# A layer of attention, scan and FFN on one core: the scan's PSUM results copied out by ACT, its rotation tables built by POOL, joined with block seams by halves and grouped transposes

## The chip, the core and the metric

The kernel runs on one core of a Trainium2 chip. A core has a matrix engine (TensorE, here PE, with its weight loads as PEld), a vector engine (VectorE, DVE), an activation engine (ScalarE, ACT), GpSimd (POOL) and a queue engine (SyncE, SP) that issues most DMAs. Each engine runs its own instructions in the order in which the program has them; semaphores hold an instruction until what it needs is done. Matmul results land in PSUM, which PE, DVE and ACT reach; everything else lies in SBUF, which all engines reach. The metric is the device time of one execution in microseconds (us), the median of several.

## The reference, cut to what matters

One layer over 2048 latent tokens and 256 context tokens of width 1024: a combined input projection gives q, k, v for a neighbourhood attention, u for a bidirectional complex-diagonal scan (S5), and two gates; both branches are merged, projected and added; an FFN follows. The part that the change touches is the scan:

```python
def s5_direction(u_ctx, u_lat, lam_re, lam_im, log_dt, b_re, b_im, c_re, c_im, reverse, need_ctx):
    lb_re, lb_im, bb_re, bb_im = s5_discretise(lam_re, lam_im, log_dt, b_re, b_im)
    def drive(u):
        u = jnp.flip(u, axis=1) if reverse else u
        return (jnp.einsum('blgh,gph->blgp', u, bb_re), jnp.einsum('blgh,gph->blgp', u, bb_im))
    def readout(hr, hi):
        y = jnp.einsum('blgp,ghp->blgh', hr, c_re) - jnp.einsum('blgp,ghp->blgh', hi, c_im)
        return jnp.flip(y, axis=1) if reverse else y
    ur, ui = drive(u_ctx)
    _, _, hc_re, hc_im = diag_scan(lb_re, lb_im, ur, ui)        # h_t = lb * h_(t-1) + u_t, complex
    h0_re, h0_im = hc_re[:, -1:], hc_im[:, -1:]
    ur, ui = drive(u_lat)
    ac_re, ac_im, hl_re, hl_im = diag_scan(lb_re, lb_im, ur, ui)
    hl_re = hl_re + ac_re * h0_re - ac_im * h0_im
    hl_im = hl_im + ac_re * h0_im + ac_im * h0_re
    return None, readout(hl_re, hl_im)
# then y = gelu(y_forward + y_backward + d_skip * u), a GLU, and the merge with the attention branch
```

There are 32 channel groups of 16 channels with 64 complex states each, in two directions. All is fp32.

## The kernel before

**Order.** The program is written stage by stage, and a scheduler sorts it when it is built: each instruction has a priority (the place in the program, shifted by `tc.cur_priority`, and raised inside `with self.hot()`), and the scheduler fills each engine's row by priority and by its own estimate of when operands are ready. The order is then fixed. `s5()` (the scan) and `attention()` have the base priority; `in_proj()` (q, k, v and gates) has 100000 more, the merge and the FFN 200000 more. So the projection is what PE gets where the scan has nothing ready, the merge what it gets under the attention.

**Projection** (`in_proj`, four blocks of 512 tokens). A weight piece is loaded by SP (`raw`), cast to a high part by ACT (L70, `whi`) and reduced to a low part by DVE (L71, `wlo`); each product is three matmuls (L92 to L94). `cols` makes one 128x512 output at a time over eight pieces of the contraction. The block's inputs `n` lie in a ring of 12 buffers, eight of them per block, loaded by SP (L357). For q and k DVE applies the rotary factors (L383 to L398). At the second block POOL builds the attention biases in the same ring (`biases`, L436 to L445): eight heads, each a load from `in_rpb`, four tensor_tensor of 128x480 and three stores.

**Scan** (`s5`). Four quarters `q` of the channels, each in two batches `sb` of four groups. A batch loads its inputs by POOL's DMA queue (L651, `ut`), lets ACT reorder them (L652, `un`), transposes them on PE (per group: the context's 32 columns twice, and two 128x128) into `ug` by an ACT copy, and builds the small matrices `win`, `cl` and `mt` on DVE, PE and ACT. Then come four steps (two pairs of groups, two directions), 32 in all. A step chunks time by 8, which leaves 288 positions, and turns the complex recurrence into a real one by rotating it:

- a table of rotation factors `er`, `ei` (128x288) grows by doubling: ACT scales (L741, L742), DVE adds (L743, L744), four times;
- PE makes the chunks' inputs `pv` in PSUM (L750, one buffer of two banks); DVE multiplies them by the table straight from PSUM (L757, L758), adds (L759, L760), runs the recurrence (L762), multiplies by the table again (L765, L766) and adds into the states `h` (L771, L772).

After four steps PE makes the outputs `py` in PSUM (L780 to L782), and ACT and DVE apply the GELU (L784 to L788; both products of DVE read `py`). After a quarter the outputs are transposed and split (L795 to L799) and stored.

## Time and profile before

| | us |
|---|---|
| median of 3 runs (3228.43 to 3234.4) | 3233.86 |
| the profiled execution | 3233.39 |
| its span, first to last instruction | 3231.6 |
| PE busy in the span | 3119.2 (97%) |
| DVE busy | 2348.4 (73%) |
| ACT busy | 1570.3 (49%) |
| POOL busy | 898.9 (28%) |

The profiled execution differs from the median by 0.5 us. Matmuls are pipelined and their ends are modelled, so a busy PE isn't PE at its peak. "Busy" counts time in which at least one instruction of the engine runs. A released-by name is inferred from semaphores. The scan's stages lie between 168 and 872 us: its first small matrices are built from 168 us on, and the last outputs are split at 872 us.

### The profile page before, as it was taken

To read this page: it belongs to the slowest core of one execution; us is meant where nothing else is said; L and a number is where in the kernel's file an instruction comes from. 1 tells how busy PE (TensorE), PEld (TensorE's weight loads), DVE (VectorE), ACT (ScalarE), POOL (GpSimd) and SP (SyncE) were. 2 spreads that over 40 slices of the span, in tenths; PEclk is the share of its full clock that TensorE was granted. 3 is DMA by queue.
4 is the path that set the end of the run, shared out by engine and by line. 5 is a ranking of instruction groups with operands and counts; after the bars stand their busy time and mean duration, and the time that the engine had idled before them with its cause. 6 is when DMAs were issued, how large, how long until landed. Compare 5 with 4: busy or idle time off the path is not lost.

```text
span 3231.6 us, 54283 instructions
## 1 busy us (share of the span) xinstructions
PE 3119.2 (97%) x20600; PEld 2727.7 (84%) x20600; DVE 2348.4 (73%) x4153; ACT 1570.3 (49%) x2746; POOL 898.9 (28%) x856
## 2 busy tenths in 40 slices
PE   7999978999999998999999999999999999999998
PEld 5987766787787778788888988888989898989988
DVE  6689787897753565665657867887858966897766
ACT  4445434454355555555554444445535543554534
POOL 2000052000223232323300544742242423341243
PEclk9999989999999999999999999999999999999999
DMA  8545567454776897987847434434344434443332
GB/s 321 186 125 172 166 194 241 163 163 140 228 211 193 268 259 213 277 238 220 254 130 269 139 126 146 141 131 147 122 136 132 150 111 131 141 147 131 112 111 101
DMA packets 212853, 564.27 MB, mean 175 GB/s; under 512 B 31785, under 2 KB 63657, under 8 KB 212593
## 3 DMA queue, kind: packets, MB, share of 16 engines
q1 hardware_dynamic: 155008, 437.48, 41.2%
q0 software_dynamic: 28032, 87.64, 10.0%
q10 hardware_dynamic: 29552, 35.70, 3.2%
q8 instruction: 162, 2.65, 0.3%
q14 instruction: 99, 0.80, 0.1%
HBM read 446.95 MB, written 111.61 MB: 173 GB/s over the span
## 4 chain that ended last, share of the span: by engine, by line
PE 79%; DVE 9%; DMA 6%; issue 3%; POOL 1%; ACT 1%; SPq 0%; ACTq 0%; DVEq 0%; POOLq 0%
PE ps L92 15%; PE ps L94 15%; PE ps L93 15%; PE ps L1068 8%; PE ps L1066 8%; PE ps L1067 8%; PE o L924 3%; DVE wlo L71 3%; PE w L884 2%; PE w L905 1%; DMA raw<-in_w_qk 1%; PE pv L750 1%; PE c L886 1%; PE c L907 1%; DVE n L1130 1%
## 5 line engine op out<-in xcount | busy, mean ns | idle before, releaser
L71 DVE TENSOR_TENSOR wlo<-raw,whi 128x1024 fp32r<-128x1024 f32 (+1 forms) x522 | 688.0, 1325 | 324.6 <-ACT whi L70 323.1
L70 ACT CAST whi<-raw 128x1024 fp32r<-128x1024 f32 (+1 forms) x522 | 508.3, 976 | 519.6 <-PE ps L94 185.8
L1066 PE MATMUL ps<-X,whi 128*128 128x256 f32 x2464 | 693.4, 284 | 13.2 <-DVE u L1078 8.4
L1068 PE MATMUL ps<-X,wlo 128*128 128x256 f32 x2464 | 692.4, 284 | 11.9 <-DVE wlo L71 11.7
L1067 PE MATMUL ps<-X,whi 128*128 128x256 f32 x2464 | 689.9, 283 | 0.0
L1066 PEld LDWEIGHTS ps<-X,whi 128*128 128x128 f32 x2464 | 471.2, 191 | 17.9 <-DVE u L1078 11.7
L1068 PEld LDWEIGHTS ps<-X,wlo 128*128 128x128 f32 x2464 | 470.5, 191 | 15.1 <-DVE wlo L71 14.9
L1067 PEld LDWEIGHTS ps<-X,whi 128*128 128x128 f32 x2464 | 471.3, 191 | 0.5
L92 PE MATMUL ps<-n,whi 128*128 128x512 f32 (+1 forms) x800 | 318.2, 398 | 10.3 <-ACT t L382 6.7
L93 PE MATMUL ps<-n,whi 128*128 128x512 f32 (+1 forms) x800 | 316.7, 396 | 0.0
L94 PE MATMUL ps<-n,wlo 128*128 128x512 f32 (+1 forms) x800 | 316.3, 396 | 0.5 <-DVE wlo L71 0.5
L92 PE MATMUL ps<-whi,zh 128*128 128x512 f32 x704 | 277.1, 395 | 0.0
L94 PE MATMUL ps<-whi,zl 128*128 128x512 f32 x704 | 277.0, 394 | 0.0
L93 PE MATMUL ps<-wlo,zh 128*128 128x512 f32 x704 | 276.9, 394 | 0.0
L1049 POOL TENSOR_TENSOR os<-raw 128x512 f32<-128x512 f32 x66 | 117.4, 1780 | 406.7 <-DMA raw<-in_w_f 330.7
L70 ACT CAST whi<-os 128x1024 fp32r<-128x1024 f32 x110 | 115.5, 1050 | 204.1 <-PE ps L1067 91.7
L71 DVE TENSOR_TENSOR wlo<-os,whi 128x1024 fp32r<-128x1024 f32 x110 | 151.3, 1376 | 62.9 <-ACT whi L70 62.9
L92 PEld LDWEIGHTS ps<-n,whi 128*128 128x128 f32 x800 | 151.3, 189 | 49.6 <-ACT t L382 9.0
L93 PEld LDWEIGHTS ps<-n,whi 128*128 128x128 f32 x800 | 151.5, 189 | 35.6 <-issue 4.1
L94 PEld LDWEIGHTS ps<-n,wlo 128*128 128x128 f32 x800 | 151.3, 189 | 35.0 <-issue 1.8
L1050 POOL TENSOR_TENSOR os<-raw,os 128x512 f32<-128x512 f32 x88 | 134.0, 1523 | 150.4 <-DMA raw<-in_w_f 148.5
L92 PE MATMUL ps<-y,whi 128*128 128x512 f32 x384 | 155.5, 406 | 5.1 <-DVE t L968 1.8
(343 smaller groups left out, 7098.8 us busy)
## 6 DMA issues: line engine op xcount, KB each, us to landing
raw<-in_w_f SPq DMA_DIRECT2D x198, 512.0 KB
raw<-sums SPq DMA_DIRECT2D x66, 512.0 KB
raw<-in_w_gate SPq DMA_DIRECT2D x64, 512.0 KB
raw<-in_w_f SPq DMA_DIRECT2D x66, 256.0 KB
raw<-in_w_qk SPq DMA_DIRECT2D x32, 512.0 KB
gsc<-e ACTq DMA_DIRECT2D x64, 256.0 KB
raw<-in_w_m SPq DMA_DIRECT2D x32, 512.0 KB
t<-gsc SPq DMA_DIRECT2D x64, 256.0 KB
```

Source lines behind the costliest of these rows:

```text
L70: self.nc.scalar.copy(hi, x)
L71: self.nc.vector.tensor_tensor(lo, x, hi.bitcast(F32), op=ALU.subtract)
L92: mm(ps, l[0], r[0], start=first, stop=False)
L93: mm(ps, l[0], r[1], start=False, stop=False)
L94: mm(ps, l[1], r[0], start=False, stop=last)
L884: nc.tensor.matmul(slv, q[:, qs], kl, start=(n == 0), stop=(n == 1))
L924: nc.tensor.matmul(o[h, g, :, hf, :], l, r, start=(n == 0), stop=(n == nb + 1), skip_group_check=True)
L1049: nc.gpsimd.tensor_tensor(s24[:, 0], s13[:, 0], a11, op=ALU.subtract)
L1050: nc.gpsimd.tensor_tensor(s24[:, 1], a12, s24[:, 0], op=ALU.subtract)
L1066: mm(dst, a[0][:, k], xh, start=(first and k == 0), stop=False, skip_group_check=True)
L1067: mm(dst, a[0][:, k], xl, start=False, stop=False, skip_group_check=True)
L1068: mm(dst, a[1][:, k], xh, start=False, stop=(k == 3), skip_group_check=True)
```

## The change

Five edits, four of them in the scan.

- The inputs `pv` leave PSUM by an ACT copy into `v`; `p1` and `p2` are then computed from `v`. The outputs `py` are copied by ACT into `yn`, and DVE's two products of the GELU read `yn`.
- The tables `er`, `ei` become one tile `ee` of two rows, and POOL builds them: one copy and sixteen tensor_tensor per step. ACT's ten and DVE's eight instructions for them go.
- The transposes of the inputs are grouped: the context's part once per group, four groups in one PSUM tile and one ACT copy that writes both ends of `ug`; the latent part of two groups in one tile and one copy.
- `cols` can take two neighbouring outputs as a pair: two weight pieces are loaded, and the first half of the contraction is done for both outputs before the second half. It is used for the first two k outputs of blocks 1 to 3, and for the last two outputs of the second gate of blocks 0 to 2.

```diff
-    def cols(self, pool, src, kt, c0, n, ops, tag="ps"):
+    def cols(self, pool, src, kt, c0, n, ops, tag="ps", pair=None):
         nm = 8 // kt
         for c in range(n):
+            if pair is not None and c == pair:
+                f = ops[0][1]
+                ws = [self.piece(src, 0, c0 + c + i, kt) for i in range(2)]
+                pss = [pool.tile([P, ops[0][0]], F32, name=tag) for _ in range(2)]
+                for h in range(2):
+                    for w, ps in zip(ws, pss):
+                        for k in range(h * kt // 2, (h + 1) * kt // 2):
+                            self.mm3(ps, (w[0][:, k], w[1][:, k]), f(k), k == 0, k == kt - 1)
+                for i, ps in enumerate(pss):
+                    yield c + i, 0, ps
+            if pair is not None and c in (pair, pair + 1):
+                continue
             w = self.piece(src, 0, c0 + c, kt)
...
-                for jj, i, ps in self.cols(pm, I["w_qk"], KD, c0, 4, ops):
+                for jj, i, ps in self.cols(pm, I["w_qk"], KD, c0, 4, ops, pair=0 if b and isk else None):
...
-                for m, _, ps in self.cols(pm, I["w_gate"], KD, gi * 8, 8, [lat]):
+                for m, _, ps in self.cols(pm, I["w_gate"], KD, gi * 8, 8, [lat], pair=6 if gi and b < NB - 1 else None):
...
+                    pt = psT.tile([P, NG, NCC], F32, name="pt")
                     for g in range(NG):
-                        pt = psT.tile([P, SEQC + NCC], F32, name="pt")
-                        nc.tensor.transpose(pt[:, 0:NCC], uc[:NCC, g], self.ident[:NCC, :NCC])
-                        for cb in range(2):
-                            nc.tensor.transpose(pt[:, NCC + cb * P:NCC + cb * P + P], un[cb][:, g], self.ident)
-                        nc.tensor.transpose(pt[:, SEQC:SEQC + NCC], uc[:NCC, g], self.ident[:NCC, :NCC])
-                        nc.scalar.copy(ug[:, g, :], pt)
+                        nc.tensor.transpose(pt[:, g], uc[:NCC, g], self.ident[:NCC, :NCC])
+                    ends = ug.rearrange("p g (n c) -> p g n c", c=NCC)[:, :, ::SEQC // NCC]
+                    nc.scalar.copy(ends, pt.unsqueeze(2).to_broadcast([P, NG, 2, NCC]))
+                    for g in range(0, NG, 2):
+                        pt = psT.tile([P, 2, 2, P], F32, name="pt")
+                        for j in range(2):
+                            for cb in range(2):
+                                nc.tensor.transpose(pt[:, j, cb], un[cb][:, g + j], self.ident)
+                        nc.scalar.copy(ug[:, g:g + 2, NCC:SEQC], pt.rearrange("p j c t -> p j (c t)"))
...
-                                er = pp.tile([P, SEQC], F32, name="er")
-                                ei = pp.tile([P, SEQC], F32, name="ei")
-                                nc.scalar.copy(er[:, 0:32], self.eb[:, 0, :, pr])
-                                nc.scalar.copy(ei[:, 0:32], self.eb[:, 1, :, pr])
+                                ee = pp.tile([P, 2, SEQC], F32, name="er")
+                                er, ei = ee[:, 0], ee[:, 1]
+                                G = nc.gpsimd
+                                G.tensor_copy(ee[:, :, 0:32], self.eb[:, :, :, pr])
                                 for i, m in enumerate((32, 64, 128, 256)):
                                     w = min(m, SEQC - m)
-                                    zr, zi, zn = (self.zz[:, i, x, pr:pr + 1] for x in range(3))
-                                    ea = pp.tile([P, P], F32, name="ea", bufs=1)
-                                    eb = pp.tile([P, P], F32, name="eb", bufs=1)
-                                    nc.scalar.activation(ea[:, :w], er[:, 0:w], AF.Copy, scale=zr)
-                                    nc.scalar.activation(eb[:, :w], ei[:, 0:w], AF.Copy, scale=zr)
-                                    V.scalar_tensor_tensor(er[:, m:m + w], ei[:, 0:w], zn, ea[:, :w], op0=ALU.mult, op1=ALU.add)
-                                    V.scalar_tensor_tensor(ei[:, m:m + w], er[:, 0:w], zi, eb[:, :w], op0=ALU.mult, op1=ALU.add)
+                                    zr, zi = (self.zz[:, i, x, pr:pr + 1].unsqueeze(1).to_broadcast([P, 2, w]) for x in range(2))
+                                    ea = pp.tile([P, 2, P], F32, name="ea", bufs=1)
+                                    G.tensor_tensor(ee[:, :, m:m + w], ee[:, :, 0:w], zr, op=ALU.mult)
+                                    G.tensor_tensor(ea[:, :, :w], ee[:, :, 0:w], zi, op=ALU.mult)
+                                    G.tensor_tensor(er[:, m:m + w], er[:, m:m + w], ea[:, 1, :w], op=ALU.subtract)
+                                    G.tensor_tensor(ei[:, m:m + w], ei[:, m:m + w], ea[:, 0, :w], op=ALU.add)
...
+                                with self.hot():
+                                    nc.scalar.copy(v, pv[:, :, 0:SEQC])
...
-                                V.tensor_tensor(p1, pv[:, :, 0:SEQC], two(er, SEQC), op=ALU.mult)
-                                V.tensor_tensor(p2, pv[:, :, 0:SEQC], two(ei, SEQC), op=ALU.mult)
+                                V.tensor_tensor(p1, v, two(er, SEQC), op=ALU.mult)
+                                V.tensor_tensor(p2, v, two(ei, SEQC), op=ALU.mult)
...
+                            yg = yn[cb][:, :, g0 + p0 * 2:g0 + p0 * 2 + 4].rearrange("p t g h -> p t (g h)")
+                            y2f = y2.rearrange("p t g h -> p t (g h)")
+                            nc.scalar.copy(yg, py.rearrange("p t g h -> p t (g h)"))
                             nc.scalar.activation(y2, py, AF.Square)
                             nc.scalar.activation(y2, y2, AF.Copy, scale=0.044715, bias=1.0)
-                            V.tensor_tensor(y2, y2, py, op=ALU.mult)
+                            V.tensor_tensor(y2f, y2f, yg, op=ALU.mult)
                             nc.scalar.activation(y2, y2, AF.Tanh, scale=math.sqrt(2.0 / math.pi))
-                            V.scalar_tensor_tensor(yn[cb][:, :, g0 + p0 * 2:g0 + p0 * 2 + 4].rearrange("p t g h -> p t (g h)"), y2.rearrange("p t g h -> p t (g h)"), 1.0,
-                                                   py.rearrange("p t g h -> p t (g h)"), op0=ALU.add, op1=ALU.mult)
+                            V.scalar_tensor_tensor(yg, y2f, 1.0, yg, op0=ALU.add, op1=ALU.mult)
```

The scheduler sorts the changed program anew, so rows move that the diff doesn't name. Three places follow.

DVE before, the end of the second batch's third step: table instructions (`er`, `ei`) stand between the scan's own (`p`, `h`) and the projection's (`qt`).

```order
L743 SCALAR_TENSOR_TENSOR er<-ei,zz,ea 128x128
L392 TENSOR_TENSOR qt<-t_5996,t_5997 128x4x2x32 x2
L744 SCALAR_TENSOR_TENSOR ei<-er,zz,eb 128x128
L765 TENSOR_TENSOR p_2740<-v,er 128x2x256
L766 TENSOR_TENSOR p_2741<-v,ei 128x2x256
L743 SCALAR_TENSOR_TENSOR er<-ei,zz,ea 128x32
L398 SCALAR_TENSOR_TENSOR qt<-qt 128x512
L744 SCALAR_TENSOR_TENSOR ei<-er,zz,eb 128x32
L771 TENSOR_TENSOR h_2750<-p_2740,p_2741 64x256
L772 TENSOR_TENSOR h_2750<-p_2740,p_2741 64x256
```

DVE now, the end of the same step.

```order
L71 TENSOR_TENSOR wlo<-raw,whi 128x1024
L782 TENSOR_TENSOR p_2740<-v,er 128x2x256
L783 TENSOR_TENSOR p_2741<-v,er 128x2x256
L404 TENSOR_TENSOR qt<-t_5758,t_5759 128x4x2x32 x2
L788 TENSOR_TENSOR h_2750<-p_2740,p_2741 64x256
L789 TENSOR_TENSOR h_2750<-p_2740,p_2741 64x256
```

The table's rows are gone, and the scan's own follow each other more closely.

POOL before, at the attention biases: only the biases and the scan's input loads (`ut`).

```order
L443 TENSOR_TENSOR n<-n,am 128x480
L445 DMA be<-n 128x2x320 x2
L445 DMA bi<-n 128x2x440
L442 TENSOR_TENSOR n<-am,n 128x480 x2
L443 TENSOR_TENSOR n<-n,am 128x480 x2
L445 DMA be<-n 128x2x320 x2
L436 DMA n<-in_rpb 128x1x960
```

POOL now, at the same place.

```order
L455 TENSOR_TENSOR n<-n,am 128x480
L457 DMA be<-n 128x2x320 x2
L758 TENSOR_TENSOR er<-er,ea 128x32
L759 TENSOR_TENSOR er<-er,ea 128x32
L457 DMA bi<-n 128x2x440
L454 TENSOR_TENSOR n<-am,n 128x480 x2
L751 COPY er<-eb 128x2x32
L756 TENSOR_TENSOR er<-er,zz 128x2x64
L757 TENSOR_TENSOR ea<-er,zz 128x2x64
L455 TENSOR_TENSOR n<-n,am 128x480
L448 DMA n<-in_rpb 128x1x960
```

The tables of the scan's steps stand in one row with the biases and the loads that these wait for.

PE before, the scan's last output transposes (`yn`): they stand among the 256-column matmuls of the last block's value projection.

```order
L93 MATMUL ps<-wlo,n 128x256
L94 MATMUL ps<-whi,n 128x256
L795 MATMUL pt<-ident,yn_4401 128x128 x8
L92 MATMUL ps<-whi,n 128x256
L93 MATMUL ps<-wlo,n 128x256
```

PE now: they stand among 512-column matmuls that come ahead of those.

```order
L93 MATMUL ps<-n,whi 128x512
L94 MATMUL ps<-n,wlo 128x512
L92 MATMUL ps<-n,whi 128x512
L814 MATMUL pt<-ident,yn_4257 128x128 x8
L93 MATMUL ps<-n,whi 128x512
L94 MATMUL ps<-n,wlo 128x512
```

The end of the scan has moved ahead in PE's row: 267 matmuls of 512 columns and 33 of 256 that stood before it stand behind it.

## Rows read from the trace of the kernel before

**Rows 1.** The page's first part: engine, busy us (share of the span), instructions.

```profile
PE 3119.2 (97%) x20600; PEld 2727.7 (84%) x20600; DVE 2348.4 (73%) x4153; ACT 1570.3 (49%) x2746; POOL 898.9 (28%) x856
```

**Rows 2.** Busy us (instructions) by stretch: PE, PEld, DVE, ACT, POOL; granted clock, DMA.

```profile
168.00:340.00 172.00, 170.65 (x1042) 142.07 (x1041) 153.76 (x335) 87.13 (x196) 8.23 (x10) 1.00 0.50 152
340.00:551.00 211.00, 183.84 (x951) 144.18 (x951) 169.09 (x300) 82.89 (x172) 67.57 (x70) 0.94 0.64 201
551.00:724.00 173.00, 172.66 (x950) 138.19 (x949) 149.49 (x298) 86.68 (x177) 4.77 (x6) 1.00 0.52 169
724.00:872.00 148.00, 148.00 (x785) 116.00 (x784) 121.01 (x239) 67.98 (x138) 14.88 (x28) 1.00 0.52 167
...
400.00:530.00 130.00, 105.61 (x570) 85.17 (x569) 109.38 (x182) 45.94 (x97) 64.46 (x66) 0.91 0.64 191
```

**Rows 3.** Waits, 388 to 560 us: engine, line, released by, total us, times, longest.

```profile
POOL n L442 <- DMA n<-in_rpb: 53.6, 7, 11.3
...
ACT un L652 <- DMA ut<-us: 18.0, 2, 10.6
...
PE pv L750 <- DVE p L758: 9.0, 2, 7.2
```

**Rows 4.** Timeline of PE in the scan: start us, us, instruction.

```profile
388.04 0.40 PE L92 MATMUL ps<-n,whi 128*128 128x512 f32 x1
...
392.24 0.40 PE L92 MATMUL ps<-n,whi 128*128 128x512 f32 x1
```

**Rows 5.** Busy time by stretch of line L743, then of L744.

```profile
168.00:872.00 704.00, 37.01 (x128) 0.98 0.55 174
...
168.00:872.00 704.00, 38.07 (x128) 0.98 0.55 174
```

**Rows 6.** Groups by line and shape, 150 to 910 us: count, busy us, mean ns.

```profile
L757 DVE TENSOR_TENSOR p<-pv,er 128x576 f32<-128x576 f32 x32 | 24.1, 753 | 1.8 <-PE pv L750 1.5
...
L765 DVE TENSOR_TENSOR p<-v,er 128x512 f32<-128x512 f32 x32 | 22.0, 686 | 0.2
```

**Rows 7.** Groups of DVE by line and shape, 400 to 530 us.

```profile
L71 DVE TENSOR_TENSOR wlo<-raw,whi 128x1024 fp32r<-128x1024 f32 x13 | 18.8, 1442 | 9.8 <-ACT whi L70 9.8
L772 DVE TENSOR_TENSOR h<-p,p 64x256 f32<-64x256 f32 x8 | 8.1, 1017 | 0.1
...
L743 DVE SCALAR_TENSOR_TENSOR er<-ei,zz,ea 128x64 f32<-128x64 f32 x5 | 2.1, 425 | 0.0
```

**Rows 8.** Groups of DVE by line and shape, 552 to 850 us.

```profile
L71 DVE TENSOR_TENSOR wlo<-raw,whi 128x1024 fp32r<-128x1024 f32 x41 | 50.1, 1221 | 17.6 <-ACT whi L70 17.2
...
L772 DVE TENSOR_TENSOR h<-p,p 64x256 f32<-64x256 f32 x32 | 13.5, 421 | 0.5
...
L743 DVE SCALAR_TENSOR_TENSOR er<-ei,zz,ea 128x64 f32<-128x64 f32 x14 | 3.9, 278 | 0.0
```

**Rows 9.** POOL's instructions by line: count, duration ns min/median/max, first and last start.

```profile
L442 POOL TENSOR_TENSOR n<-am,n x16: 1188/1347/2334, 408.4 to 520.9; 128x480 f32<-128x480 f32 x16
L443 POOL TENSOR_TENSOR n<-n,am x16: 991/1106/1974, 411.2 to 523.4; 128x480 f32<-128x480 f32 x16
...
L178 POOL COPY sel<-ident x1: 176/176/176, 2.3 to 2.3; 2x2 f32<-2x2 f32 x1
```

**Rows 10.** Timeline of DVE, then of POOL, from 423 us.

```profile
423.11 0.69 DVE L387 TENSOR_TENSOR t<-t,t 128x512 f32<-128x512 f32 x1
423.72 0.44 DVE L708 TENSOR_TENSOR cl<-p 64x288 f32<-64x288 f32 x1
424.18 1.39 DVE L709 SCALAR_TENSOR_TENSOR cl<-p 64x288 f32<-64x288 f32 x1
...
423.81 2.83 POOL L442 TENSOR_TENSOR n<-am,n 128x480 f32<-128x480 f32 x2 [7.09 <-DMA n<-in_rpb]
```

**Rows 11.** Groups of DVE by line and shape, 1800 us to the end.

```profile
L1085 DVE TENSOR_TENSOR n<-u 128x256 f32<-128x256 f32 x88 | 48.8, 555 | 3.0
L1088 DVE TENSOR_TENSOR n<-ps,u 128x256 f32<-128x256 f32 x88 | 36.9, 419 | 12.3 <-PE ps L1068 12.2
```

## The prediction, made before the changed kernel ran

> **What bounds the kernel now.** I read the busy shares first. TensorE (PE) is busy 97% of the span [rows 1], so time can only come from stretches where PE waits, or where its instruction order sends it to something that isn't ready. Next I cut the span into stages. The scan runs from 168 to 872 us, and I take its four passes over the channel quarters as four stretches [rows 2]. In the first, third and fourth PE is busy all the time: the projection's matmuls fill every gap of the scan. DVE is busy 154 of 172, 149 of 173 and 121 of 148 us there. In the second PE is idle for 27 us (183.8 of 211) and GpSimd (POOL) is busy for 68. The waits of that stretch say why: POOL builds the attention biases, stands 53.6 us on their loads, and the scan's input loads are queued behind; ACT then stands 18 us on those inputs [rows 3], and all its copies for the projection with it. So in the scan PE and DVE are both near their limit, and the order decides how much projection stands inside the scan. After 872 us nothing of this change runs.
>
> **The tables leave DVE.** Per scan step (32 of them) eight scalar_tensor_tensor of DVE build the table er, ei. Together they are busy 37.0 + 38.1 = 75.1 us [rows 5]. All go. Back-to-back DVE instructions overlap by up to 0.08 us (423.11 + 0.69 against the next start at 423.72 [rows 10]), 20 us for 256 of them, so the time that comes free is 55 to 75 us; I take 60. ACT loses ten instructions per step as well; it waits rather than bounds, so I count nothing.
>
> **The scheduler then moves projection out of the scan.** Counted in the order on PE, between the first transposes of the scan's inputs and its last output transposes there stood 1752 matmuls of 512 columns and 753 of 256; now 1485 and 720. A 512-column matmul starts 0.233 us after the one before (18 of them in 4.20 us, from 388.04 to 392.24 [rows 4]). 267 x 0.233 = 62 us, and 33 at about half of it 4 us: **66 us of projection now stand behind the scan**, where PE has no gap of that size. On DVE 12 weight pieces (1.22 us each [rows 8]) and 19 rotary instructions (0.69 us, as the 512-element row [rows 6]) go with them, 28 us. So the new order only pays if the scan gets 66 us shorter. If it stays as long as it was, the kernel is 66 us longer.
>
> **The tables on POOL.** Per step there is one small copy, eight tensor_tensor over 2w and eight over w elements, with w = 32, 64, 128 and 32: 1024 elements against a broadcast factor and 512 plain ones. The nearest POOL rows are 480 elements wide: 1.19 us with two plain operands, 0.99 us at best with one broadcast, and a 2-element copy takes 0.18 [rows 9]. With no fixed part: 1024 x 0.99/480 + 512 x 1.19/480 + 0.1 = 3.5 us. With 0.18 us fixed in each: 16 x 0.18 + 1024 x 0.81/480 + 512 x 1.01/480 + 0.25 = 5.9 us. No row is nearer to either end, so I take the middle, 4.7 us, 150 us in all (112 to 189). POOL had little to do in the scan, so as a load this is hidden.
>
> **What it costs DVE.** It isn't hidden from DVE. At 424 us a DVE instruction on 288 elements takes 1.39 us while POOL's tensor_tensor runs beside it; the one before, of the same size, took 0.44 [rows 10]. In the stretch with the biases, 400 to 530 us, eleven DVE groups read longer than in the undisturbed 552 to 850: from the weight rest, 13 x (1.442 - 1.221) = 2.9 us, and the h instructions of L772, 8 x (1.017 - 0.421) = 4.8, down to 5 x (0.425 - 0.278) = 0.7 for the table's 64-wide ones [rows 7, 8]. They add up to 19 us, for 16 x (1.19 + 0.99) = 35 us of undisturbed POOL work [rows 9]: 0.56 us of DVE for each us on POOL. Which instructions? Late in the kernel, 256-element ones whose inputs both lie in SBUF read 0.555 us, and those with one input in PSUM 0.419 [rows 11]; only the first are slowed. The change moves exactly such instructions over: p1 and p2 (L757, L758) and the two products of the GELU read PSUM now and will read SBUF alone. It gains nothing for it in the instruction itself: 0.753 us for 576 elements from PSUM and 0.686 for 512 from SBUF [rows 6] lie on one line, 0.15 us + 1.04 ns per element. DVE was at its own work for 69% of that stretch ((109.4 - 19.4)/130 [rows 2]); in the scan it will be more, with hardly a PSUM operand left. I take 0.65: 150 x 0.65 = 98 us; ends 112 x 0.56 = 63 and 189 x 0.9 = 170.
>
> The Trainium skill, "SBUF — State Buffer", section "Who interferes with whom", speaks against the change in the same place: a DVE instruction with two SBUF inputs and a GpSimd instruction that reads SBUF take one shared port in turn, and whichever starts first blocks the other completely. The rows agree on which operands are hit; on how much they show 0.56 and not 1, since DVE isn't always there to be blocked. By the rule at its face all 150 us would be DVE's loss; that is a rival below.
>
> **The copies and the rest.** p1 and p2 now wait for an ACT copy of pv (an estimate of 0.6 us, 32 times, from the 0.69 us that DVE takes for a row of that size [rows 6]); the rest of DVE's queue, weight rests included, waits behind them, and ACT's own queue behind the copy. In exchange pv's single PSUM buffer comes free without DVE (PE waited 9.0 us for that, in two waits of the second pass [rows 3]). I count 0, between -9 and +20 (32 x 0.6). The grouped transposes take 32 small ones off PE; at less than a 512-column matmul's 0.233 us each that is under 7 us, and lies in a stage that DVE ends. The seams by halves let three block ends release, and three block starts use, half of the ring first, but hold two accumulators at once; the trace names no PE wait on the ring's loads in the scan's stretches, so I count 0, within 8 either way.
>
> **The sum.** DVE's busy time in the scan was 153.8 + 169.1 + 149.5 + 121.0 = 593 us of 704. Now 593 - 60 - 25 (the 28 less overlaps) = 508, plus 98 = 606. DVE reached 0.89 of its stretch at best (153.8 of 172), 0.84 on average. With less projection per step it is what ends last, so I take 0.89: 606/0.89 = 681 us for the scan. The change of time is 681 - 704 + 66 = **+43 us**, less some 3 for the transposes: +40. The profiled execution took 3233.39 us outside its 3231.6 us span, beside a median of 3233.86, so I add to the median: **3274 us**. The ends of the collisions and of the utilization give (508 + 63)/0.95 = 601, that is 601 - 704 + 66 = -37 or 3197 us, and (508 + 170)/0.88 = 770, +132 or 3366 us. A difference under 0.2% (6 us) can't be told from none here.
>
> **Rivals.**
> *It does what the order assumes*: the collisions are few and PE bounds the scan. PE was busy 675 us in the four stretches; less 66 and 5 that is 604. Then 604 - 704 + 66 = -34: 3200 us. For it: PE was busy all the time in three of four stretches. It decides when collisions cost under 75 us or so. Chance 0.24.
> *The lock at full price*: each us of a POOL table is a us of DVE. (508 + 150)/0.89 = 739, +101: 3335 us. For it: the 1.39 us rows, where DVE waits out POOL and POOL then waits out DVE. Against it: 0.56 on the mean. Chance 0.14.
> *POOL's queue*: POOL takes its work in order, and three tables begin between the first bias and the last, behind their loads; the scan's input loads stand in the same row. POOL was busy 64.5 us in 400 to 530 and stood 53.6 on loads there [rows 2, 3]: 118 of 130 us. With four tables in it (19 us, longer by POOL's own waits for the lock) it doesn't fit, and DVE waits some 25 us for a table or for its inputs. On top of the forecast: 3299 us. Chance 0.10.
> *Nothing measurable*: the scan shrinks by just the 66 us. 3234 us, chance 0.08.
>
> **How the numbers follow.** The forecast's own chance is 0.44. Slower: 0.44 + 0.14 + 0.10 = 0.68; same 0.08; faster 0.24. The range runs from 3200, which leaves out half of the first rival (0.12), to 3335, which leaves out half of the second (0.07).
>
> **What would show it.** The scan's last output transposes near 168 + 681 = 849 us (it is 872 now, and 772 by the first rival); the two h instructions at 0.6 us and more instead of 0.42 throughout the scan; L71's mean above 1.3 us there; PE idle some 11% of the scan instead of 4%, its waits put down to pv, py or the projection's copies; POOL tables of 5 to 10 us. If the h instructions stay at 0.42, the collision step is wrong; if the scan ends at 772 us with them lengthened, DVE wasn't what ends last; and if the time behind the scan doesn't grow by 66 us, the step on the moved projection is wrong.

## The result and the profile after

The changed kernel takes 3248.75 us (3245.68 to 3253.46), the kernel before in the same runs 3232.14: 1.0059 times, interval 1.0043 to 1.0075. It is **16.6 us slower**; the forecast was 40 slower, in a range that holds 3249.

The profiled execution spans 3243.9 us, 12.3 more than before. First the page's busy row, then busy us by stretch (PE, PEld, DVE, ACT, POOL; granted clock, DMA share, GB/s) for the four passes of the scan and for the 828 us behind it, as [rows 1, 2].

```profile
PE 3116.8 (96%) x20568; PEld 2730.0 (84%) x20568; DVE 2366.3 (73%) x3897; ACT 1510.9 (47%) x2466; POOL 1223.2 (38%) x1400
```

```profile
168.00:324.00 156.00, 139.39 (x871) 118.08 (x870) 145.81 (x241) 56.11 (x91) 107.33 (x175) 0.94 0.45 131
324.00:486.00 162.00, 145.91 (x777) 116.25 (x775) 137.10 (x201) 57.48 (x86) 96.06 (x146) 0.94 0.46 149
486.00:673.00 187.00, 166.22 (x834) 130.78 (x835) 156.92 (x219) 65.47 (x98) 135.87 (x203) 0.94 0.63 204
673.00:834.00 161.00, 154.76 (x871) 124.03 (x870) 143.91 (x224) 66.25 (x101) 79.33 (x127) 0.99 0.57 175
834.00:1662.00 828.00, 810.60 (x5403) 673.01 (x5402) 472.96 (x1084) 443.30 (x804) 220.08 (x364) 0.99 0.77 233
```

In [rows 2] three passes had PE busy all the time at clock 1.00. Now it is idle in all of them, 60 of 666 us (29 of 704 before), and the granted clock is 0.94 in three, so part of them ran at the lower of its two levels (1.2 GHz). DVE is busy 584 of 666 us.

The scan's last output transposes, in the kernel before and in the changed one (count, ns min/median/max, first and last start):

```profile
L795 PE MATMUL pt<-ident,yn x16: 270/272/273, 860.3 to 868.2; 128*128 128x128 f32 x16
```

```profile
L814 PE MATMUL pt<-ident,yn x8: 271/272/273, 830.7 to 831.4; 128*128 128x128 f32 x8
```

The scan ends 37 us earlier (868.5 to 831.7), and from there to the end it takes 2412.2 us instead of 2363.1, **49 us more**. The difference is the 12.3. In PE's order 1552 matmuls of 512 columns and 1632 of 256 of the projection stand ahead of the last of these transposes, 1824 and 1665 before: 272 x 0.233 us and 33 at half of that, **67 us**, were moved behind. So the scan is 700.5 - 67 = 633.5 us of old work, about 4 less for the 32 transposes that are gone (e4's scan below is 6 us shorter than what was moved out of it), and took 663.7: **34 us too long**. And the stretch behind took 18 us less than what it had and got.

Waits of PE in the changed scan, 168 to 834 us (total us, times, longest):

```profile
PE py L799 <- DVE h L789: 24.5, 11, 7.5
PE ps L92 <- ACT t L394: 10.4, 3, 5.2
PE pv L765 <- ACT v L768: 7.3, 1, 7.3
PE py L798 <- DVE h L789: 6.5, 5, 4.2
```

PE now waits 31 us for the states h, which it didn't before. And this is DVE's work by shape in the same stretch (count, busy us, mean ns, idle before it):

```profile
L71 DVE TENSOR_TENSOR wlo<-raw,whi 128x1024 fp32r<-128x1024 f32 x76 | 101.9, 1341 | 27.2 <-ACT whi L70 22.2 <-PE pt L814 4.4
L779 DVE TENSOR_TENSOR_SCAN v<-r,v 128x288 f32<-128x288 f32 x64 | 51.1, 833 | 0.0
L789 DVE TENSOR_TENSOR h<-p,p 64x256 f32<-64x256 f32 x64 | 35.5, 554 | 0.9
L788 DVE TENSOR_TENSOR h<-p,p 64x256 f32<-64x256 f32 x64 | 32.8, 512 | 1.7
...
L775 DVE TENSOR_TENSOR p<-v,er 128x576 f32<-128x576 f32 x32 | 26.6, 831 | 0.1
L774 DVE TENSOR_TENSOR p<-v,er 128x576 f32<-128x576 f32 x32 | 25.3, 791 | 24.9 <-POOL er L758 21.4 <-ACT v L768 2.0
```

The h instruction read 421 ns undisturbed [rows 8], p 753 [rows 6]; all are longer now, and DVE waits 21.4 us for tables. POOL's own instructions are lengthened more (ns min/median/max):

```profile
L751 POOL COPY er<-eb x32: 282/540/1354, 166.9 to 793.3; 128x64 f32<-128x64 f32 x32
...
L756 POOL TENSOR_TENSOR er<-er,zz x128: 282/624/1547, 167.4 to 800.7; 128x64 f32<-128x64 f32 x64, 128x128 f32<-128x128 f32 x32, 128x256 f32<-128x256 f32 x32
```

The fastest instances of the seventeen add up to 5.9 us a table; as run it is 10.5 (335 us for 32).

### The profile page after: what moved, and what is told of

Its sections match the earlier page's. It is cut to its first block, busy times and chain, and to the rows that moved or that the text cites. A ratio compares the mean times of both kernels' runs of the same rounds, so it can differ in the third digit from the quotient of the medians.

```text
span 3243.9 us, 54121 instructions
## 1 busy us (share of the span) xinstructions
PE 3116.8 (96%) x20568; PEld 2730.0 (84%) x20568; DVE 2366.3 (73%) x3897; ACT 1510.9 (47%) x2466; POOL 1223.2 (38%) x1400
## 4 chain that ended last, share of the span: by engine, by line
PE 63%; DVE 7%; DMA 3%; POOL 2%; issue 2%; ACT 1%; SPq 0%; POOLq 0%; DVEq 0%; ACTq 0%
PE ps L92 11%; PE ps L94 11%; PE ps L93 11%; PE ps L1087 8%; PE ps L1085 8%; PE ps L1086 7%; PE o L943 3%; DVE wlo L71 3%; PE w L903 2%; PE w L924 2%; PE c L905 1%; PE c L926 1%; DMA y<-as 1%; DMA raw<-in_w_gate 1%; DVE n L1149 0%
## 5 line engine op out<-in xcount | busy, mean ns | idle before, releaser
L71 DVE TENSOR_TENSOR wlo<-raw,whi 128x1024 fp32r<-128x1024 f32 (+1 forms) x522 | 695.9, 1340 | 315.6 <-ACT whi L70 309.1
L71 DVE TENSOR_TENSOR wlo<-os,whi 128x1024 fp32r<-128x1024 f32 x110 | 150.7, 1370 | 65.4 <-ACT whi L70 65.4
```

The lines of the kernel that those rows point to most:

```text
L71: self.nc.vector.tensor_tensor(lo, x, hi.bitcast(F32), op=ALU.subtract)
```

## The experiments

Every order differs, so each run is read in three numbers beside its time. **Moved**: (1824 - count) x 0.233 us and (1665 - count) x 0.117 us, the counts being the projection's matmuls of 512 and of 256 columns ahead of the scan's last output transpose. **Excess**: the scan, from 168 us to that transpose, against 700.5 less moved (and less 4 with grouped transposes). **Rest**: how much the stretch behind differs from 2363.1 plus moved. The expectations count ahead of the first of the last sixteen transposes (1814 before, 1514 in the changed kernel, 70 us), which gives 1 to 5 us more moved, in e14 9. The ratio is against the kernel before in the same runs.

Excess and rest come from the one profiled execution, whose time stands beside the median. It is 11 us above the median in e6 and 13 below it in e7, and the kernel before ran from 3221 to 3246 us beside e1 to e4; so differences of some 10 us in these two columns mean little.

| run | us | profiled | ratio, interval | moved | excess | rest |
|---|---|---|---|---|---|---|
| changed | 3248.75 | 3245.7 | 1.0059 (1.0043-1.0075) | 67 | 34 | -18 |
| e1 tables back | 3223.77 | 3222.4 | 0.9972 (0.9955-0.9988) | 30 | -6 | -1 |
| e2 8 tables on POOL | 3241.26 | 3238.1 | 1.0019 (1.0005-1.0034) | 80 | 1 | 7 |
| e3 operands in PSUM again | 3241.61 | 3242.4 | 1.0023 (1.0009-1.0037) | 28 | 16 | -3 |
| e4 seams, transposes alone | 3233.99 | 3240.3 | 1.0003 (0.9986-1.0020) | 18 | -2 | 13 |
| e5 before + idle tables | 3286.58 | 3278.8 | 1.0160 (1.0138-1.0182) | -3 | 50 | -5 |
| e6 16 tables on POOL | 3257.85 | 3269.3 | 1.0079 (1.0062-1.0097) | 45 | 19 | 21 |
| e7 copy of pv, no GELU copy | 3238.51 | 3225.6 | 1.0010 (0.9997-1.0023) | 18 | -9 | 5 |
| e8 both copies alone | 3251.18 | 3249.3 | 1.0046 (1.0029-1.0062) | 26 | 10 | 6 |
| e9 changed, strip single | 3269.95 | 3267.5 | 1.0113 (1.0094-1.0132) | 49 | 27 | 11 |
| e10 tables back, strip single | 3226.36 | 3230.0 | 0.9979 (0.9969-0.9988) | 30 | -2 | 2 |
| e11 three table buffers | 3253.38 | 3252.9 | 1.0059 (1.0041-1.0076) | 66 | 33 | -10 |
| e12 e10 + idle tables | 3320.58 | 3320.4 | 1.0263 (1.0243-1.0282) | 26 | 88 | 3 |
| e13 changed, directions swapped | 3266.04 | 3266.3 | 1.0096 (1.0078-1.0114) | 9 | 34 | 3 |
| e14 changed, halves of py swapped | 3284.34 | 3280.4 | 1.0150 (1.0129-1.0170) | 23 | 36 | 15 |
| e15 changed, pairs swapped | 3259.75 | 3264.2 | 1.0076 (1.0058-1.0095) | 27 | 34 | 1 |
| e16 before, strip single | 3256.18 | 3256.0 | 1.0062 (1.0046-1.0078) | -3 | 0 | 22 |
| e17 e10, input loads by SP | 3255.18 | 3254.1 | 1.0057 (1.0043-1.0072) | 38 | 3 | 21 |
| e18 e17 + idle tables | 3294.04 | 3294.0 | 1.0180 (1.0161-1.0199) | 38 | 44 | 21 |

### The parts of the change: e1, e3, e4, e7, e8

e1 puts the tables of the kernel before (L743, L744 there) into the changed kernel:

```diff
-                                ee = pp.tile([P, 2, SEQC], F32, name="er")
...
-                                G.tensor_copy(ee[:, :, 0:32], self.eb[:, :, :, pr])
...
+                                nc.scalar.copy(er[:, 0:32], self.eb[:, 0, :, pr])
+                                nc.scalar.copy(ei[:, 0:32], self.eb[:, 1, :, pr])
...
+                                    V.scalar_tensor_tensor(er[:, m:m + w], ei[:, 0:w], zn, ea[:, :w], op0=ALU.mult, op1=ALU.add)
```

> The changed kernel with the rotation tables built on ACT and DVE again, as before; copies to SBUF, seams and grouped transposes stay. In the order 1668 512-column matmuls of the projection stand ahead of the scan's last outputs (before 1814, changed 1514), so some 34 us are moved behind the scan instead of 70. Theory (POOL's tables slow the DVE instructions that read two SBUF operands): the tables' 75 us come back to DVE, the 63 us of collisions go, the h instructions fall back to 0.42-0.45 us, the scan takes 685-700 us and the whole about 3240 us. Rival (the ACT copies and the waits on them are what holds the scan): the time stays at 3249 us or rises, since the copies are all there and DVE has more to do.

Measured 3224, faster than both kernels, 16 us better than expected; the rival falls. DVE in its scan:

```profile
L780 DVE TENSOR_TENSOR_SCAN v<-r,v 128x288 f32<-128x288 f32 x64 | 46.7, 747 | 0.1
L790 DVE TENSOR_TENSOR h<-p,p 64x256 f32<-64x256 f32 x64 | 28.6, 446 | 0.9
...
L775 DVE TENSOR_TENSOR p<-v,er 128x576 f32<-128x576 f32 x32 | 24.1, 754 | 4.9 <-ACT v L769 4.8
L776 DVE TENSOR_TENSOR p<-v,ei 128x576 f32<-128x576 f32 x32 | 24.1, 753 | 0.0
```

The same instructions, the same copies, and the durations are back, h at 446 and 431 ns but for the biases' share. p reads SBUF in 754 ns as it read PSUM in 753, as the prediction had it, and waits 4.8 us for the copy in all.

e3 puts p and the GELU back on PSUM:

```diff
-                                V.tensor_tensor(p1, v, two(er, SEQC), op=ALU.mult)
+                                V.tensor_tensor(p1, pv[:, :, 0:SEQC], two(er, SEQC), op=ALU.mult)
```

> The changed kernel with p1, p2 and the GELU's products reading PSUM again (no ACT copy); tables on POOL, seams and grouped transposes stay. In the order 1688 512-column matmuls stand ahead of the scan's last outputs (29 us behind the scan against before, 70 in the changed kernel). Theory (only DVE instructions with two SBUF operands collide): p1 and p2 read 0.75 us and aren't lengthened, collisions fall from 63 to some 40 us, DVE in the scan is 593 - 60 + 40 - 10 = 563 us; PE is then what ends last at about 650 us, and the whole takes 3205-3215 us. Rival (every DVE instruction collides, or POOL's queue is what holds): p1 and p2 lengthen to 0.9 us and more, the time stays at 3245-3260 us.

```profile
L777 DVE TENSOR_TENSOR_SCAN v<-r,v 128x288 f32<-128x288 f32 x64 | 53.4, 869 | 0.1
...
L772 DVE TENSOR_TENSOR p<-pv,er 128x576 f32<-128x576 f32 x32 | 24.2, 756 | 15.8 <-POOL er L758 13.0 <-PE pv L765 0.8 <-issue 0.5
L773 DVE TENSOR_TENSOR p<-pv,er 128x576 f32<-128x576 f32 x32 | 23.9, 747 | 0.0
```

With all POOL tables running, p from PSUM stays at 756 and 747 ns while the recurrence beside it, with both inputs in SBUF, reads 869. So instructions with two SBUF inputs collide, one with an input in PSUM doesn't, and the move to SBUF made that worse: excess 16 here, 34 with it (27 to 36 in the orders below; e3 itself is one order). The time, 3242, missed the expected 3205 to 3215.

e4 leaves only the seams and the transposes, e7 adds the copy of pv, e8 is both copies without seams and transposes.

> The kernel before with the seams by halves and the grouped transposes alone; tables on ACT and DVE, p1, p2 and GELU from PSUM. In the order 1728 512-column matmuls stand ahead of the scan's last outputs, 86 fewer than before: 20 us more behind the scan. Theory (these two edits change no duration): the scan's 704 us shrink by 10-20 us with what left it, and the whole takes 3230-3242 us. Rival (the seams cost PE waits, since two accumulators are held at once): PE waits at the blocks' seams, 3250 us or more, and this alone is the changed kernel's loss.

> Tables back on ACT and DVE, seams and grouped transposes, and of the copies to SBUF only that of pv: the GELU's products read PSUM again. In the order 1728 512-column matmuls stand ahead of the scan's last outputs (20 us moved). If the copy of pv is what made the kernel with the tables back faster than the one with seams and transposes alone (3224 against 3234 us), 3224-3227 us; if it is the copy of the outputs, 3233-3236 us.

> The kernel before with the copies of pv and py to SBUF alone: tables on ACT and DVE, no seams, no grouped transposes. In the order 1689 512-column matmuls stand ahead of the scan's last outputs (29 us moved). If the copies are what is worth something, 3224-3229 us; if the seams and the transposes are, the time of before, 3231-3236 us. Theory: the copies free the two PSUM buffers early and cost DVE nothing, 3227 us.

e4 came as expected. e7 gave 3239, e8 3251, both outside what I expected, and neither names a part that gains. The 10 us between e4 and e1 are no more than the orders below differ by.

### The number of tables: e2, e6, e11

e2 builds the table ahead of the loop over p0, once per batch; e6 uses POOL `if d:` and ACT and DVE otherwise; e11 has `name="er", bufs=3`.

> The changed kernel with 8 tables instead of 32: POOL builds one per batch of four groups, for the first step, and the four steps of the batch share it (24 tables are left out, the result is not the reference's). DVE's instructions and all copies are the same. In the order 1452 512-column matmuls stand ahead of the scan's last outputs, 62 fewer than in the changed kernel (14 us more behind the scan). Theory (collisions): three quarters of 63 us go, 47 us of DVE; the h instructions read 0.45 us or less, the scan takes 615-630 us, the whole about 3215 us. Rival (copies and waits): the scan only gets shorter by the 14 us that the order takes out, 3245-3250 us.

> The changed kernel with the tables of the second direction on POOL and those of the first on ACT and DVE as before: 16 tables instead of 32. In the order 1610 512-column matmuls stand ahead of the scan's last outputs (48 us moved, 70 in the changed kernel, 34 with all tables back). Theory (each POOL table lengthens the scan by the same amount; with 32 the scan was 41 us longer than the matmuls that left it explain, with 8 it was 9 us, with none 2 us): 20 us here, the scan takes 665-675 us and the whole lies between the two, 3232-3242 us. Rival (POOL is only too late while it has more than it can do, so that half of them are free): the scan takes 650 us, the whole 3220-3226 us, as with no table on POOL.

> The changed kernel with three table buffers instead of two, so that POOL may work a step further ahead (to make room strip is single and the 128-wide doubling is done in two halves of 64, 20 tensor_tensor a table instead of 16). 1521 512-column matmuls stand ahead of the scan's last outputs. Theory (DVE's instructions get longer beside POOL's): DVE's 21 us of waits for a late table go, but the collisions stay or grow; the scan stays some 30 us longer than its order. Rival (the tables come late because POOL's own instructions are lengthened, and that is what holds the scan): the excess of the scan falls under 15 us, and the whole is 20 us or more faster than the changed kernel with strip single.

Excess 1, 19 and 34 for 8, 16 and 32 tables (e6's text counts without the 4 us of the transposes): it grows with their number. e2 and the changed kernel are the clean pair, since in both DVE has no table work; in e6 it builds half of them. The times don't follow: e2 gave 3241 instead of 3215, e6 3258 instead of at most 3242. Their rests are 7 and 21, the changed kernel's is -18, and 11 of e6's 21 are its profiled execution. In e11 DVE still waits 13 us for tables and the excess stays at 33: POOL's head start doesn't heal it. The 17 us by which e11 is faster than e9 lie in the rest.

### The same work in other orders: e9, e10, e13 to e16

The spread asked for this. e9, e10 and e16 make one small buffer single in the changed kernel, in e1 and in the kernel before; e13 to e15 write two iterations in the other order. The scheduler then sorts anew.

```diff
-                        strip = bp.tile([16, 2, 240], F32, name="strip", bufs=2)
+                        strip = bp.tile([16, 2, 240], F32, name="strip", bufs=1)
...
-                            for d in range(2):
+                            for d in (1, 0):
```

> The changed kernel with one small buffer (strip) single instead of double: the same work, but the planner sets another order. 1592 512-column matmuls of the projection stand ahead of the scan's last outputs (52 us moved behind the scan against before; 70 in the changed kernel). In the changed kernel the time behind the scan grew by 48 us only, 22 less than moved. Theory: those 22 us are chance of the order; the scan is 38 us longer than its order, the rest of the kernel grows by the 52 us that were moved, and the whole takes 3258-3270 us. Rival: work moved behind the scan always gets part of its time back there (a third), because it fills waits of attention and merge; then 3245-3252 us, as the changed kernel.

> The changed kernel with all tables back on ACT and DVE, and strip single: the same work as the first experiment in another order (some 170 of 18446 rows of PE stand elsewhere; 1669 512-column matmuls ahead of the scan's last outputs against 1668). It shows how much time the order alone moves: theory 3220-3240 us, 3224 us with strip double. Rival: the gain of the copies to SBUF is a gain of the work, then 3221-3227 us.

> The changed kernel with the two directions of a pair of groups written in the other order: the same work, another order. 1753 512-column matmuls stand ahead of the scan's last outputs (14 us moved, 70 in the changed kernel). Theory (the tables on POOL make the scan 31-38 us longer than its order, whatever is moved; the rest is chance of about 10 us): 3252-3275 us, the middle 3263. Rival (what is moved behind the scan decides the loss): with 14 us moved the time of before, 3235 us.

> The changed kernel with the two halves of the outputs py written in the other order: the same work, another order; 32 us moved. Theory: 3252-3275 us, the middle 3263. Rival (a return of a third of what is moved): 3256 us and below the one with 14 us moved.

> The changed kernel with the two pairs of groups of a GELU written in the other order: the same work, another order; 32 us moved. Theory: 3252-3275 us, the middle 3263. With the changed kernel (3249) and the one with strip single (3270) this gives five orders of the same work.

> The kernel before with strip single: the same work, some 600 rows of PE stand elsewhere, 1817 512-column matmuls ahead of the scan's last outputs (1814 before). The control for the run with idle tables. Theory: 3225-3245 us, so that the 3287 us with idle tables are theirs. Rival (a single strip costs what the idle tables seemed to): 3260 us and more.

Five orders of the changed work: 3249, 3260, 3266, 3270, 3284, mean 3266. Their excess is 27 to 36 with 9 to 67 us moved, so it doesn't come from what was moved. e14's 3284 and e16's 3256 lie outside what I expected: the order is worth some 15 us either way, in the kernel before too. The changed kernel is the best of its five, by its rest of -18. Busy us of 828 behind the scan, of before and of e9 (the changed kernel's row is above):

```profile
872.00:1700.00 828.00, 798.52 (x5465) 671.12 (x5465) 470.57 (x1087) 445.21 (x827) 219.53 (x361) 0.98 0.77 229
```

```profile
843.00:1671.00 828.00, 789.08 (x5211) 655.38 (x5210) 461.49 (x1057) 430.56 (x779) 222.55 (x367) 0.97 0.77 229
```

PE idles 29 us, 39 in e9, and 17 in the changed kernel, at clocks 0.98, 0.97 and 0.99. The longest of these waits in before, in the changed kernel and in e9:

```profile
PE ps L92 <- ACT whi L70: 14.8, 4, 6.5
```

```profile
PE w L924 <- ACT s L917: 3.3, 4, 1.5
...
PE ps L92 <- ACT whi L70: 2.9, 1, 2.9
```

```profile
PE ps L92 <- ACT whi L70: 9.0, 2, 5.2
PE ps L92 <- DMA y<-ys: 7.0, 1, 7.0
```

They are waits of attention and merge on weights and inputs, none on anything the change touches. One of them, PE's wait for weights that ACT casts, is 12 us shorter in the changed kernel than before (14.8 to 2.9), and by 12 us PE idles less in these 828 us. Whether much moved work helps there isn't settled: with 66 to 80 us moved the rest is -10, -18 and 7, with less it is -5 to 22.

### Contention by itself: e5, e12, e17, e18

POOL builds a table of 240 columns in each step that nobody reads:

```diff
+                                eg = pp.tile([P, 2, 240], F32, name="eg", bufs=1)
...
+                                G.tensor_copy(eg[:, 0, 0:32], er[:, 0:32])
+                                G.tensor_copy(eg[:, 1, 0:32], ei[:, 0:32])
+                                for i, (m, w) in enumerate(((32, 32), (64, 64), (128, 112), (192, 32))):
...
+                                    G.tensor_tensor(eg[:, :, m:m + w], eg[:, :, 0:w], zr, op=ALU.mult)
...
```

This is e18's; e5 and e12 start from `eb` and so can run ahead.

> The kernel before, with all its work, and beside it POOL builds in every scan step a further table of 240 columns (one copy and sixteen tensor_tensor, 94% of the elements of the changed kernel's table) that nobody reads; to make room, one small buffer (strip) is single. The order of PE hardly moves: 1817 512-column matmuls stand ahead of the scan's last outputs, before 1814. Theory (a POOL table slows the DVE instructions beside it, and the scan gets longer for it): some 45 us of collisions on DVE, PE waits for h, the scan is 20-40 us longer and the whole 3255-3270 us. Rival (the loss is only in the matmuls that the planner moved behind the scan): nothing is moved, 3230-3237 us.

> All tables back on ACT and DVE, strip single, copies to SBUF, seams and transposes as in the changed kernel, and beside them POOL builds in every step a 240-column table that nobody reads. 1694 512-column matmuls stand ahead of the scan's last outputs, 25 more than without the idle tables. Nothing waits for these tables, so what they cost is their contention alone. Theory: as on the kernel before (52 us there), 3265-3285 us, 40-55 us over the same kernel without them. Rival (only the wait for a table costs, not the contention): the time of the kernel without them, within 8 us.

e12 gave 94 us over e10 and e5 30 over its control e16, but not by contention alone. ACT's waits for the scan's input loads in e12 (in e5 they are 78.3 us, in its control 29.5):

```profile
ACT un L664 <- DMA ut<-us: 79.7, 14, 35.8
```

The loads stand in POOL's queue behind the idle tables. So e17 issues them from SP, and e18 adds tables that can't run ahead.

> Tables back on ACT and DVE, strip single, and the scan's input loads issued by SP instead of POOL: nothing of the scan stands in POOL's queue. 1641 512-column matmuls stand ahead of the scan's last outputs (40 us moved). It is the base of the next run: 3226 us as with the loads on POOL, within the 15 us that the order alone moves.

> The same with idle tables of POOL in every step (two small copies from the step's own first columns and sixteen tensor_tensor on 240 columns; nobody reads them); again 1641 matmuls ahead of the scan's last outputs. No load waits behind them. Theory (contention on DVE): the h instructions read 0.5 us and more, and the scan gets 35-55 us longer, the whole 30-60 us over the run without them. Rival (the cost of the idle tables was the queue of the input loads): within 15 us of the run without them.

The scan of e17, then of e18, and p in e18:

```profile
168.00:830.00 662.00, 618.48 (x3473) 500.92 (x3472) 576.61 (x1141) 334.31 (x702) 75.79 (x83) 0.97 0.56 172
```

```profile
168.00:870.00 702.00, 634.15 (x3478) 507.80 (x3477) 628.62 (x1142) 336.08 (x704) 400.19 (x659) 0.95 0.53 163
```

```profile
L786 DVE TENSOR_TENSOR p<-v,ei 128x576 f32<-128x576 f32 x32 | 27.0, 843 | 0.0
L785 DVE TENSOR_TENSOR p<-v,er 128x576 f32<-128x576 f32 x32 | 26.5, 829 | 6.0 <-ACT v L779 6.0
```

ACT's waits for the inputs in e18:

```profile
ACT un L664 <- DMA ut<-us: 8.9, 10, 1.7
```

Same moved work, same rest, no load behind a table: DVE is busy 52 us longer, the scan takes **40 us** more (662 to 702), the whole 39 (3255 to 3294). The h instructions didn't lengthen here (471 and 460 ns in means), a miss: other instructions met the tables. e17, the base, missed its 3226: it is 29 us slower than e10, 19 of it in the rest, where its edit changes nothing: the order again.

One wait for POOL is left in e18. Its copies read `er`, ACT may write that buffer again only behind them, and at the biases POOL was late:

```profile
ACT er L750 <- POOL eg L763: 27.4, 1, 27.4
```

It doesn't make the 40 us. The first p of a scan step starts 3 us later than in e17 at the first step, 20 at the sixteenth, 22 at the seventeenth, which is the next one behind this wait, and 44 at the last: e17 loses about as much time between these two steps (94 us against 96), and the 40 us gather over all the others.

## Why the prediction was half right

**Right: the mechanism and the scan.** Its sum let the scan lose 66 and get 43 of it back (681 - 704 + 66). The measured excess is 34, in five orders 27 to 36, mean 33; tables that nobody reads gave 40. *Nothing measurable* and *it does as the order assumes* fall with it. *The lock at full price* falls: the scan would have taken its 739 us, and took 664. *POOL's queue*: ACT waits 25.1 us on the inputs in the changed scan, 30.3 before, so the tables didn't hold the loads up here; e12 shows the queue can cost much when tables run ahead. DVE's 21.4 us of waits for tables belong partly to this rival, which I had priced at 25 for the batch with the biases alone.

**Its inner terms were off and made up for one another, so that the scan's sum came out near is in part luck.** A table is 5.9 us undisturbed, not 4.7: the end of my bounds with a fixed part in each instruction. Collisions: each shape's mean while POOL works against its median without adds to 81 us in the changed scan, 64 with p and the GELU on PSUM (e3), 25 in e1, all of that at the biases. So the tables cost DVE 56 us, not 98: 56/189 = 0.30 of a us per undisturbed us of POOL, not 0.65. I had taken the price from the biases' 480-element instructions; at the tables' short ones POOL lost 4.6 us a table and DVE 1.8. DVE's 584 us in the scan (forecast 606) over 666 are 0.88 (forecast 0.89). Of the 22 us less, 42 are collisions; some 20 the other way I can't place.

**The step that failed: "66 us of projection now stand behind the scan, where PE has no gap of that size".** 67 us were moved, and the time behind grew by 49. That stretch is not a constant plus what is added: it is sorted anew too, and it had gaps. PE's busy time from the scan's end to the last instruction, before and in the changed kernel (second and third number):

```profile
868.50:3231.60 2363.10, 2296.96 (x15719) 2057.62 (x15717) 1653.00 (x2615) 1167.91 (x1940) 782.62 (x725) 0.99 0.54 170
```

```profile
831.70:3243.90 2412.20, 2361.66 (x16024) 2108.46 (x16023) 1678.32 (x2643) 1187.36 (x1967) 780.34 (x725) 0.99 0.54 171
```

PE got the 305 matmuls and 65 us of work, but was idle 51 us there instead of 66. The sum had no term for that; it needed one of 15 us either way. That this order got time back is luck: in the four other orders of the same work the rest is 1 to 15, and the mean of the five, 3266, is 8 us from the forecast. The step is 17 us (66 against 49) of the gap of 28 in the profiled executions (forecast 40, measured 12); the other 11 are the scan, 37 us earlier where forecast and transposes gave 26.

**What would show it.** The last transposes at 831 us, not 849. h at 0.51 and 0.55 us, under the 0.6 that I named. L71 at 1.34, over 1.3 as said. PE idle 9% of the scan (said 11), waiting for py first, as said. A table 10.5 us, just over 5 to 10. The time behind didn't grow by 66, the sign I had named for that step being wrong.

The Trainium skill, "SBUF — State Buffer", section "Who interferes with whom", has the shared port blocked whole by whoever starts first. On the operands the runs agree (p from SBUF 753 ns without tables on POOL and 831 with them, from PSUM 747 with them). By the rule at its face DVE would lose up to the tables' 189 us; it lost 56, and POOL's tables took 146 longer than undisturbed.

**The remedy** is e1: without POOL's tables 3224 and 3226 in two orders that differ little, 0.2 to 0.3% under the kernel before. The kernels without work added on POOL lie between 3224 and 3256 by order, so that this is a gain of the copies isn't shown.

## What to carry over

Before moving elementwise work to GpSimd, look at which of VectorE's instructions read two SBUF operands: they pay, and taking others off PSUM at the same time adds to those that pay. When a scheduler sorts the program, split a result into the stage and the rest, and run the same work in three or four orders before believing a difference of half a per cent: here one order was worth 15 us, as much as the change.

## What was not expected

The price of contention isn't one number: 56 us for 189 of short instructions on 32 to 256 elements, but 20 for 35 us of the biases' on 480 (in the kernel before). And a single small buffer, of no use to anything late, moved the kernel before by some 23 us (3233 to 3256), 19 of them behind the scan, where that buffer is no longer used.
